# Hybrid attention and SSM block: attention's gate projection z moved from the head loop into two token-major passes

## The chip, the cores and the metric

The kernel runs on one core of one Trainium2 chip. The metric is the device time of one execution in microseconds; several runs are taken and their median is given. Beside it stands one profiled execution, whose trace is read here. Engines: PE is TensorE's matrix products, PEld its weight loads, DVE is VectorE, ACT is ScalarE, POOL is GpSimd, SP is SyncE, which issues most DMAs.

## The reference

One layer over 256 tokens of width 2048, in fp32. The normed input `hn` is projected by `w_in` to q, k, v, a gate `z_a`, and the inputs of a state-space branch (SSM). Attention has 16 heads of 128 with three dilated patterns and ALiBi slopes; the attended output is gated by `silu(z_a)` and projected.

```python
hn = rms_norm(x, norm_w)
proj = hn @ w_in
q, k, v, z_a, z_s, xbc, dt_raw, g_a, g_s = jnp.split(proj, split_points, axis=-1)
...
o_a = jnp.einsum('pbsh,pbshe->bshe', wts.astype(q.dtype), jnp.stack(outs))
o_a = o_a.reshape(b, s, ATTN_WIDTH) * jax.nn.silu(z_a)
...
y = rms_norm(y * jax.nn.silu(z_s), ssm_norm_w)
merged = jax.nn.sigmoid(g_a) * (o_a @ w_attn_branch) + jax.nn.sigmoid(g_s) * (y @ w_ssm_branch)
return x + merged @ w_out
```

A last RMS norm follows.

## The kernel before

**Precision by splitting.** Every fp32 operand of a large product is split into a high part (ScalarE copies it into the matmul's reduced format, `h`) and a low part (VectorE subtracts, `l`). A product is then high x high, high x low and low x high, accumulated in one PSUM bank. Weights come from HBM in units of 128 x 1024 fp32 (512 KB), in an order laid out by `weight_plan`; `unit` splits a unit (lines 278 and 279) into rings of four `h` and four `l` tiles, and the raw units have a ring of five. `XT` holds the transposed input with its high and low parts side by side (256 + 256 columns), 16 blocks (`KT`) of 128 rows.

**Two forms of projection.** `gemm_a` makes 128 output columns feature-major: the weight block is the stationary operand, `XT` streams. For each of the 16 blocks it issues one product of 512 columns (the high weight with both parts of the input, line 333) and one of 256 (the low weight with the high part, line 339). `gemm_pair` makes 1024 output columns token-major for both halves of the tokens: `XT` is stationary, weights stream 512 wide, and it works by quads, two blocks of 128 rows at a time. A plain quad has 24 products of 512 columns (lines 484 to 486, in `triple`). A quad listed in `S_QUADS` uses seven block products instead of eight (Strassen's way), 21 products, for which VectorE makes sums and differences of the weight blocks (`wt`, `wa`), unless an earlier "presum" job has put them in memory (`sum_jobs`: three markers on POOL, two loads on SP, two VectorE subtractions at lines 254 and 255, one store on SP). Products go to four banks of their own (`pp_`), the plain ones to four others (`ps_`), which swap between the passes c = 0 and c = 2; `fold` (lines 589 to 594) adds them together at the end.

**Stages, in order.** A first stage with the norm; eight SSM groups (xs, zs, B and C by `gemm_a`, with weight presums and left-operand sums made ahead); the SSM branch's output product (`ssm`, two `gemm_pair` passes); v (two passes); the loop over 16 heads; the gate `ga` (two passes); `attn` and `out` (two passes each); the last norm. In the head loop each head has three `gemm_a` projections, q, k and `za`. Their results are brought out of PSUM by `evac`, and `half_silu` makes the gate.

**The order of the work.** A clock of ticks (one for each projection, or each quad) says when the small steps are issued: `after(ticks, f)` puts a step on a list and `tick` runs what is due. For a head: `scores` (line 1051, then softmax on VectorE and ScalarE), `turn_p` (three 128x128 transposes of p on TensorE, line 1075), `mix` (p times v, lines 1082 and 1083, result feature-major, times the gate, split into `oaT`). A scheduler that simulates the engines puts the program's instructions in order; instructions marked with `in_order` keep theirs, among them the first and last product of each q, k and za projection. `oaT` is the left operand of `attn`; `keep_left` makes the sums of its seven-product quads.

**Memory.** Large areas are reused under tags: `yo0a`, `yo0b`, `yo1a`, `yo1b`. The SSM outputs `yT` lie in all four. During v, `yo0a` gives room for weight sums and `yo0b` for four extra split tiles (`tl`); `yo1b` becomes `th_a`, in which the attention stage's presum jobs work and later the gate `ga`.

Of the kernel before, what the change touches and what calls it, by code (L numbers as in the profile page):

```python
# [9 lines left out]
F32 = mybir.dt.float32  # L10
# [5 lines left out]
P = 128  # L16
S = 256
# [30 lines left out]
IN_TWOS = {(n, t) for n in ("xs", "zs") for t in range(4)} | {("B", 1), ("B", 4)} | {(n, h) for n in ("q", "k", "za") for h in range(2)}  # L48
# [35 lines left out]
def weight_plan():  # L84
# [114 lines left out]
def hybrid_block(ctx: ExitStack, tc: tile.TileContext, wall, xt, x, pk_d, cst_d, fw_d, out):  # L199
# [95 lines left out]
    def kt_of(t, kt):  # L295
        return t[kt // 8][:, kt % 8, :] if isinstance(t, list) else t[:, kt, :]

    def two_kts(t, q):
        t, q = (t[q // 4], q % 4) if isinstance(t, list) else (t, q)
        return t[:, 2 * q : 2 * q + 2, :]  # L300

# [135 lines left out]
    def fetch_left(kept, pool, bufs, key, x, spare, u, queue=nc.sync):  # L437
        def get(behind):
            sx = new_sx(pool, bufs, spare, f"{key[0]}{key[1]}")
            gp.tensor_copy(sx[:, 0, 0, 0:1], behind)  # L440
            queue.dma_start(sx.bitcast(F32), lefts[key])
            kept[key[1]] = left_parts(sx, x, spare)

        behind_unit(u, get)
# [24 lines left out]
    def gemm_pair(tag, x_of, n_kt, sxs, swap, extra={}, close=1, order=None, room={}, tail=None):  # L469
# [22 lines left out]
        for at, q in enumerate(order):  # L492
# [6 lines left out]
            if q not in quads:  # L499
# [8 lines left out]
                if tail and at == n_q - 1:  # L508
# [6 lines left out]
                for (ae, k, h, l), i, c, acc, cs, start, stop in jobs:  # L515
                    triple(acc, *ae[i][k], h[:, c, cs], l[:, c, cs], start=start, stop=stop and at == n_q - 1)
# [107 lines left out]

    yT = [half_kts(f"yT{n}", f"yo0{n}") for n in "ab"]
    ssq = cpool.tile([P, 2, S], F32, name="ssq", tag="ssq")
# [388 lines left out]

    def open_gate(c, es, prods):
        dst = blocks(th_a, c)
        fold(prods, dst)
        for d, e in zip(dst, es):
            ve.tensor_tensor(d, e, d, ALU.add)  # L1020
            ac.activation(d, d, AF.Tanh, scale=0.5)

    vt = big.tile([P, 2, D], F32, name="vt", tag="yo1a")
    th_a = big.tile([P, 2, D], F32, name="th_a", tag="yo1b")
    xl = ctx.enter_context(tc.tile_pool(name="xl", bufs=1))
# [18 lines left out]
    with tc.tile_pool(name="att", bufs=2) as ap:  # L1044
        ev = ap

        oaT = [half_kts("oaTa", "yo0a")]

# [28 lines left out]

        def mix(h, pT, za):
            ops = bank("m2", 2, f"ops{h}")
            o = za  # L1080
            hs = slice(h * P, (h + 1) * P)
            pe.matmul(ops[:, :S], vt[:, 0, hs], pT[:, :S], start=True, stop=False)
            pe.matmul(ops[:, P:S], vt[:, 1, hs], pT[:, S:384], start=False, stop=True)
            ve.tensor_tensor(o, ops[:, :S], za, ALU.mult)
            if h == 8:
                oaT.append(half_kts("oaTb", "yo0b"))
            split(o, kt_of(oaT, h)[:, :S], kt_of(oaT, h)[:, S:])
# [4 lines left out]
        sum_jobs(  # L1092
            SUMS_ATT, [FIRST[("q", 0)] + 3 + n * 15 // 4 for n in range(len(SUMS_ATT))],
            [
# [5 lines left out]
        for h in range(NH):  # L1100
# [5 lines left out]
            pT = ap.tile([P, 384], F32, name=f"pT{h}", tag="pT", bufs=1)  # L1106
            za = ap.tile([P, S], F32, name=f"za{h}", tag="za", bufs=3)
            after(S_LAG + (6, 4, 2)[max(h - 13, 0)], lambda a=(h, pT, za): mix(*a))
            after(S_LAG + (3 if h < 15 else 1), lambda a=(h, p, pT): turn_p(*a))
            after(S_LAG + (h == 0), lambda a=(h, q, k, p): scores(*a))  # L1110
            zh = ev.tile([P, S], F32, name=f"zah{h}", tag="eh", bufs=2)
            evac(project(("za", h)), zh, f"za{h}", scale=0.5)
            half_silu(zh, za, f"za{h}")

        for n, q in enumerate(ATT_QUADS):
            fetch_left(
                sx_of_o, xl if n else xk, max(1, n and len(SX_X) - 1), ("o", q), two_kts(oaT, q), 0, FIRST[("ga", 2)] + O_BEHIND[n], nc.gpsimd
            )
# [8 lines left out]
    with tc.tile_pool(name="fin", bufs=2) as fp:  # L1127
# [42 lines left out]

        fw = big.tile([P, D], F32, name="fw", tag="yo0b")
        for n, (tag, u) in enumerate(FW_BEHIND):
            cs = slice(n * UNIT, (n + 1) * UNIT)
            behind_unit(
                FIRST[tag] + u, lambda behind, cs=cs: fetch(fw[:, cs], fw_d[cs].partition_broadcast(P), behind, nc.scalar)
            )
# [9 lines left out]
        for c0 in (0, 2):  # L1186
# [17 lines left out]
            for i in range(2):  # L1204
                f = fs[:, i, :9]
                for c, acc in zip((c0, c0 + 1), es[2 * i : 2 * i + 2]):
# [17 lines left out]
                    if (c, i) == (2, 1):  # L1224
                        y2 = y
                    else:
                        ve.tensor_tensor(fin[:, i, cs], y, fw[:, cs], ALU.mult)
                    if c == 1:
# [7 lines left out]
        for i in range(2):  # L1236
            r = fs[:, i, 7:8]
            for c in (3, 0, 2, 1) if i else (3, 0, 1, 2):
                cs = slice(c * 512, (c + 1) * 512)
                if i and c == 2:  # L1240
                    ve.scalar_tensor_tensor(fin[:, i, cs], y2, r, fw[:, cs], ALU.mult, ALU.mult)
                elif c == 0 or c == (1 if i else 3):
# [40 lines left out]
```

## Time and profile before

| | |
|---|---|
| median of 3 runs | 1380.61 us (1380.14 to 1382.33) |
| profiled execution | 1379.87 us |
| its span | 1378.0 us |
| PE busy | 1366.8 us, 99% |
| DVE busy | 1177.0 us, 85% |
| ACT busy | 840.0 us, 61% |
| HBM | 252 GB/s over the span |

The span runs from the first to the last instruction of the trace. Matmuls are pipelined: the next starts before one has ended, so a duration in the trace is longer than the distance between two starts. The chain of waits is the chain of work that ended last, followed back from the last instruction; a piece of it is the time by which that instruction moved the end.

### The profile page before, as it was taken

The numbers are of one execution on the slowest core, as the hardware profiler recorded it, in microseconds if no ns is written. First come the engines' busy times: TensorE is split into PE (matmuls) and PEld (weight loads), VectorE is DVE, ScalarE is ACT, GpSimd is POOL, SyncE is SP. The second block draws the span as 40 slices with busy tenths as digits, with TensorE's granted clock in tenths as the row PEclk, the third lists the DMA queues.
The fourth block names the chain that finished last, engine by engine and source line by source line (L and its number), as shares of the span: only waits on it lengthen the run. The fifth ranks groups of instructions, "written<-read, shape, count | busy, mean of one in ns | idle before, by whom it ended". The sixth has DMA issues, their size and how long they took to land.

```text
span 1378.0 us, 20734 instructions
## 1 busy us (share of the span) xinstructions
PE 1366.8 (99%) x7260; PEld 1164.8 (85%) x7260; DVE 1177.0 (85%) x1763; ACT 840.0 (61%) x1310; POOL 161.7 (12%) x238
## 2 busy tenths in 40 slices
PE   9999999999999999999999999999999999999997
PEld 7888888888888888888888888888888888888886
DVE  6898899898899888788989888777877789988897
ACT  7655777675667676666565554454444557655564
POOL 2301211101020100010001001211211000400112
PEclk9999999999999999999999999999999999999999
DMA  9767878778787867578677568888889757875773
GB/s 342 237 190 237 298 267 286 262 244 288 248 277 237 298 203 220 174 242 277 228 261 270 211 215 316 306 275 280 306 298 302 230 163 267 291 244 173 246 273 122
DMA packets 106520, 348.15 MB, mean 253 GB/s; under 512 B 11888, under 2 KB 14256, under 8 KB 106416
## 3 DMA queue, kind: packets, MB, share of 16 engines
q1 hardware_dynamic: 104400, 340.67, 74.0%
q10 hardware_dynamic: 1440, 4.06, 0.8%
q0 software_dynamic: 576, 2.10, 0.4%
q8 instruction: 57, 0.93, 0.3%
q14 instruction: 47, 0.39, 0.1%
HBM read 316.97 MB, written 29.82 MB: 252 GB/s over the span
## 4 chain that ended last, share of the span: by engine, by line
PE 98%; DMA 0%; DVE 0%; ACT 0%; issue 0%; SPq 0%; POOL 0%; POOLq 0%; DVEq 0%
PE ps_xs L333 8%; PE ps_zs L333 8%; PE ps_k L333 4%; PE ps_za L333 4%; PE ps_q L333 4%; PE ps_zs L339 4%; PE ps_xs L339 4%; PE ps_ssm L485 3%; PE ps_ssm L486 3%; PE ps_ssm L484 3%; PE ps_q L339 2%; PE ps_za L339 2%; PE ps_k L339 2%; PE ps_gs L421 2%; PE ps_gs L422 2%; PE ps_gs L420 2%
## 5 line engine op out<-in xcount | busy, mean ns | idle before, releaser
L278 ACT ACTIVATE h<-w 128x1024 fp32r<-128x1024 f32 (+1 forms) x394 | 410.0, 1048 | 306.0 <-issue 73.7
L279 DVE TENSOR_TENSOR l<-w,h 128x1024 fp32r<-128x1024 f32 (+1 forms) x394 | 474.0, 1209 | 111.1 <-ACT h L278 106.9
L333 PE MATMUL ps_zs<-XT,h 128*128 128x512 f32 x496 | 172.0, 393 | 0.0
L333 PE MATMUL ps_xs<-XT,h 128*128 128x512 f32 x496 | 171.6, 393 | 0.0
L339 PE MATMUL ps_zs<-XT,l 128*128 128x256 f32 x496 | 134.6, 279 | 0.0
L339 PE MATMUL ps_xs<-XT,l 128*128 128x256 f32 x496 | 133.7, 277 | 0.0
L333 PEld LDWEIGHTS ps_xs<-XT,h 128*128 128x128 f32 x496 | 91.3, 188 | 19.4
L333 PEld LDWEIGHTS ps_zs<-XT,h 128*128 128x128 f32 x496 | 91.3, 188 | 18.9
L339 PEld LDWEIGHTS ps_zs<-XT,l 128*128 128x128 f32 x496 | 93.3, 188 | 2.1
L339 PEld LDWEIGHTS ps_xs<-XT,l 128*128 128x128 f32 x496 | 93.2, 188 | 2.1
L333 PE MATMUL ps_q<-XT,h 128*128 128x512 f32 x256 | 91.1, 404 | 0.0
L333 PE MATMUL ps_k<-XT,h 128*128 128x512 f32 x256 | 88.6, 395 | 0.0
L333 PE MATMUL ps_za<-XT,h 128*128 128x512 f32 x256 | 88.4, 394 | 0.0
L551 ACT ACTIVATE ha<-wa 128x1024 fp32r<-128x1024 f32 x45 | 47.5, 1056 | 45.9 <-PE ps_ssm L486 10.0
L339 PE MATMUL ps_q<-XT,l 128*128 128x256 f32 x256 | 68.4, 278 | 0.0
L339 PE MATMUL ps_k<-XT,l 128*128 128x256 f32 x256 | 68.4, 277 | 0.0
L339 PE MATMUL ps_za<-XT,l 128*128 128x256 f32 x256 | 68.4, 277 | 0.0
L552 DVE TENSOR_TENSOR la<-wa,ha 128x1024 fp32r<-128x1024 f32 x45 | 54.8, 1218 | 8.4 <-ACT ha L551 8.3
L552 DVE TENSOR_TENSOR ltu<-wa,htu 128x1024 fp32r<-128x1024 f32 x40 | 48.7, 1219 | 10.8 <-ACT htu L551 10.8
L793 ACT ACTIVATE gt<-acb,acT 128x128 f32<-128x128 f32 x128 | 44.1, 390 | 22.2 <-DMA acb<-acum_d 21.9
L333 PEld LDWEIGHTS ps_k<-XT,h 128*128 128x128 f32 x256 | 47.0, 188 | 9.9
L333 PEld LDWEIGHTS ps_q<-XT,h 128*128 128x128 f32 x256 | 47.1, 188 | 9.7
(691 smaller groups left out, 3347.8 us busy)
## 6 DMA issues: line engine op xcount, KB each, us to landing
w<-in_wall SPq DMA_DIRECT2D x390, 512.0 KB, 4.8
wa<-in_wall SPq DMA_DIRECT2D x45, 512.0 KB, 4.7
th_a<-in_wall SPq DMA_DIRECT2D x21, 512.0 KB, 4.7
sums_at<-in_wall SPq DMA_DIRECT2D x18, 512.0 KB, 5.0
acb<-acum_d SPq DMA_DIRECT2D x32, 256.0 KB, 3.8
t_ssm<-sums_at SPq DMA_DIRECT2D x13, 512.0 KB, 4.3
wt<-t_ssm SPq DMA_DIRECT2D x13, 512.0 KB, 4.7
th_a<-in_wall SPq DMA_DIRECT2D x21, 256.0 KB, 5.4
```

What stands on the lines that cost most here:

```text
L278: ac.activation(h[:, a:b], w[:, a:b], AF.Copy)
L279: ve.tensor_tensor(l[:, a:b], w[:, a:b], h[:, a:b].bitcast(F32), ALU.subtract)
L333: high = pe.matmul(acc, h[:, kk, :], xs_of(kt), start=(kt == 0), stop=False)
L339: low = pe.matmul(acc[:, S:], l[:, kk, :], xs_of(kt)[:, :S], start=False, stop=(kt == KT - 1))
L420: pe.matmul(accs[i], xh, h[:, kk], start=(kt == 0), stop=False)
L421: pe.matmul(accs[i], xh, l[:, kk], start=False, stop=False)
L484: pe.matmul(acc, xh, h, start=start, stop=False)
L485: pe.matmul(acc, xh, l, start=False, stop=False)
L486: pe.matmul(acc, xl, h, start=False, stop=stop)
L551: ac.activation(h, src, AF.Copy)
L552: ve.tensor_tensor(l, src, h.bitcast(F32), ALU.subtract)
L793: ac.activation(g4[:, n, b], acb[:, j, b // 2 * P : b // 2 * P + P], AF.Relu, scale=-1.0, bias=sc[:, h : h + 1],)
```

## The change

The z projection leaves the head loop. It becomes two `gemm_pair` passes of 1024 columns behind v (tag `za`, c = 0 and 2), each with two seven-product quads (2 and 5) without presums. At the end of a pass VectorE adds the banks, ScalarE takes the Tanh, and VectorE writes z(1 + tanh(z/2)) token-major into four tiles `za` of four heads each. In the head loop only q and k are projected. `mix` now takes p as the stationary operand and gives the output token-major, in three products of 128 columns; VectorE multiplies by the gate; a new step `turn_o` turns the two 128x128 blocks of the head by TensorE and splits the result into `oaT`. The four steps of a head have new ticks (`ATT_LAGS`).

Around it: quad 3 of the first ga pass becomes plain and the orders of quads change; six presum jobs of ga move from the head loop to the SSM groups (four jobs a group instead of three), 14 remain in the head loop; the area `yo0b` is cut into quarters, for `yTb`, three of the `za` tiles, the second half of `oaT` and `fw`; the extra split tiles `tl` move from `yo0b` to `yo1b`; `th_a` is allocated behind the z passes; a plain quad may run due steps half way.

```diff
+ATT_LAGS = (
+    ((2, 0), (5, 0), (6, 0), (7, 0)), ((2, 0), (4, 0), (5, 0), (6, 0)),
+    ((2, 0), (3, 0), (4, 0), (5, 0)), ((1, 1), (2, 1), (3, 0), (3, 1)),
+)
+Z_ORDERS = {c: (0, 2, 1, 3, 5, 4, 6, 7) for c in (0, 2)}
-G_ORDERS = {c: (0, 2, 4, 1, 3, 5, 6, 7) for c in (0, 2)}
+G_ORDERS = {0: (0, 1, 3, 2, 4, 5, 6, 7), 2: (0, 2, 4, 1, 3, 5, 6, 7)}
-    ("v", 0): (2, 3, 4, 5, 6), ("v", 2): (2, 4, 5, 6), ("ga", 0): (2, 3, 4, 5, 6), ("ga", 2): (2, 3, 4, 5, 6),
+    ("v", 0): (2, 3, 4, 5, 6), ("v", 2): (2, 4, 5, 6), ("za", 0): (2, 5), ("za", 2): (2, 5), ("ga", 0): (2, 4, 5, 6), ("ga", 2): (2, 3, 4, 5, 6),
+N_EARLY = 6
-SUMS_SSM = [(t, q) for t in (("ssm", 0), ("ssm", 2), ("v", 0), ("v", 2)) for q in S_QUADS[t] if (t[1], q) not in IN_PLACE.get(t[0], ())]
-SUM_UNITS = 2, 9, 16
+SUMS_SSM = [(t, q) for t in (("ssm", 0), ("ssm", 2), ("v", 0)) for q in S_QUADS[t] if (t[1], q) not in IN_PLACE.get(t[0], ())]
+SUMS_SSM += SUMS_ATT[:N_EARLY]
+SUM_UNITS = 2, 7, 12, 17
...
+    for c in (0, 2):
+        pair(("za", c), "w_in", OFF_ZA + c * 512, KT)
     for h in range(NH):
         cols(("q", h), "w_in", OFF_Q + h * P, KT)
         cols(("k", h), "w_in", OFF_K + h * P, KT)
-        cols(("za", h), "w_in", OFF_ZA + h * P, KT)
...
+                for at_job, ((ae, k, h, l), i, c, acc, cs, start, stop) in enumerate(jobs):
+                    if at_job == 4:
+                        run_due(now[0] + 0.5)
...
-    yT = [half_kts(f"yT{n}", f"yo0{n}") for n in "ab"]
+    yT = [half_kts("yTa", "yo0a"), [quarter("yTb", n) for n in range(4)]]
...
-    tl = big.tile([P, 4, UNIT], F32R, name="tl_v", tag="yo0b")
+    tl = big.tile([P, 4, UNIT], F32R, name="tl_v", tag="yo1b")
...
+        for c in (0, 2):
+            es, prods = gemm_pair(
+                ("za", c), lambda kt: XT[:, kt, :], KT, sx_of_x, c == 2, order=Z_ORDERS[c], room=room
+            )
+            tmp = [mul.tile([P, UNIT], F32, name=f"z_{t}{c}", tag=t, bufs=2) for t in ("ht", "lt")]
+            dst = [t[:, n * 512 : n * 512 + 512] for t in tmp for n in range(2)]
+            fold(prods, dst)
+            for n, (d, e) in enumerate(zip(dst, es)):
+                ve.tensor_tensor(d, e, d, ALU.add)
+                ac.activation(e, d, AF.Tanh, scale=0.5)
+                four = lambda t: t.rearrange("p (h m) -> p h m", h=4)
+                ve.scalar_tensor_tensor(za[c + n % 2][:, :, n // 2], four(e), 1.0, four(d), ALU.add, ALU.mult)
+        th_a = big.tile([P, 2, D], F32, name="th_a", tag="yo1b")
...
-            pe.matmul(ops[:, :S], vt[:, 0, hs], pT[:, :S], start=True, stop=False)
-            pe.matmul(ops[:, P:S], vt[:, 1, hs], pT[:, S:384], start=False, stop=True)
-            ve.tensor_tensor(o, ops[:, :S], za, ALU.mult)
+            pe.matmul(ops[:, :P], pT[:, :P], vt[:, 0, hs], start=True, stop=True)
+            pe.matmul(ops[:, P:S], pT[:, P:S], vt[:, 0, hs], start=True, stop=False)
+            pe.matmul(ops[:, P:S], pT[:, S:384], vt[:, 1, hs], start=False, stop=True)
+            o = za[h // 4][:, h % 4].rearrange("p i s -> p (i s)")
+            ve.scalar_tensor_tensor(o, ops[:, :S], 0.5, o, ALU.mult, ALU.mult)
+
+        def turn_o(h):
+            if h in (8, 10, 12, 14):
+                oaT[1].append(quarter("oaTb", h // 2 - 4))
+            tp = bank("m2", 2, f"otp{h}")
+            for i in range(2):
+                pe.transpose(tp[:, i * P : (i + 1) * P], za[h // 4][:, h % 4, i], ident)
+            split(tp[:, :S], kt_of(oaT, h)[:, :S], kt_of(oaT, h)[:, S:])
...
-            after(S_LAG + (6, 4, 2)[max(h - 13, 0)], lambda a=(h, pT, za): mix(*a))
-            after(S_LAG + (3 if h < 15 else 1), lambda a=(h, p, pT): turn_p(*a))
-            after(S_LAG + (h == 0), lambda a=(h, q, k, p): scores(*a))
-            zh = ev.tile([P, S], F32, name=f"zah{h}", tag="eh", bufs=2)
-            evac(project(("za", h)), zh, f"za{h}", scale=0.5)
-            half_silu(zh, za, f"za{h}")
+            for (ticks, inside), f in zip(ATT_LAGS[max(h - 12, 0)], ...):
+                after(ticks, f, inside)
```

More of the change, by code (lines that the diff above doesn't have):

```diff
@@ L1045, in hybrid_block, with open_gate @@
         ev = ap
-        oaT = [half_kts("oaTa", "yo0a")]
+        za = [
+            big.tile([P, 4, 2, P], F32, name=f"za{n}", tag=f"yo0b{n}") if n < 3
+            else ap.tile([P, 4, 2, P], F32, name=f"za{n}", tag="za", bufs=1)
+            for n in range(4)
+        ]
+        for c in (0, 2):
[11 more added lines that the diff above has]
+        th_a = big.tile([P, 2, D], F32, name="th_a", tag="yo1b")
+        oaT = [half_kts("oaTa", "yo0a"), []]
+        def open_gate(c, es, prods):
+            dst = blocks(th_a, c)
+            fold(prods, dst)
+            for d, e in zip(dst, es):
+                ve.tensor_tensor(d, e, d, ALU.add)
+                ac.activation(d, d, AF.Tanh, scale=0.5)
         def scores(h, q, k, p):
@@ L1106, in hybrid_block @@
             pT = ap.tile([P, 384], F32, name=f"pT{h}", tag="pT", bufs=1)
[L1107 to L1113 removed]
+            for (ticks, inside), f in zip(
+                ATT_LAGS[max(h - 12, 0)],
+                (
+                    lambda a=(h, q, k, p): scores(*a), lambda a=(h, p, pT): turn_p(*a),
+                    lambda a=(h, pT): mix(*a), lambda h=h: turn_o(h),
+                ),
+            ):
+                after(ticks, f, inside)
         for n, q in enumerate(ATT_QUADS):
             fetch_left(
[L1117 removed]
+                sx_of_o, xl if n else xk, max(1, n and len(SX_X) - 1), ("o", q), lambda q=q: two_kts(oaT, q), 0, FIRST[("ga", 2)] + O_BEHIND[n], nc.gpsimd
             )
@@ L1169, in hybrid_block, with fw @@
             )
-        fw = big.tile([P, D], F32, name="fw", tag="yo0b")
+        fws = [big.tile([P, UNIT], F32, name=f"fw{n}", tag=f"yo0b{n}") for n in range(2)]
+        def fw(c):
+            return fws[c // 2][:, c % 2 * 512 : c % 2 * 512 + 512]
         for n, (tag, u) in enumerate(FW_BEHIND):
```

35 lines of the change are left out of this document (15 added, 20 removed).

## The prediction

> **What bounds the kernel now.** I read the profile in this order: the page's engine totals and its chain, then the busy time by stretch, then the chain of waits piece by piece where TensorE does the work that the change replaces, and last VectorE's groups and waits in the stages that get more work.
>
> ```profile
> span 1378.0 us, 20734 instructions
> PE 1366.8 (99%) x7260; PEld 1164.8 (85%) x7260; DVE 1177.0 (85%) x1763; ACT 840.0 (61%) x1310; POOL 161.7 (12%) x238
> PE 98%; DMA 0%; DVE 0%; ACT 0%; issue 0%; SPq 0%; POOL 0%; POOLq 0%; DVEq 0%
> 30.00:1360.00 1330.00, 1329.98 (x7072) 1133.51 (x7071) 1144.12 (x1709) 811.68 (x1257) 152.38 (x216) 1.00 0.76 253
> 165.00:225.00 60.00, 60.00 (x368) 52.12 (x366) 57.62 (x97) 42.91 (x82) 9.83 (x18) 1.00 0.85 289
> 225.00:285.00 60.00, 60.00 (x368) 52.08 (x366) 55.50 (x95) 42.06 (x80) 9.51 (x16) 1.00 0.80 271
> 744.00:822.00 78.00, 78.00 (x345) 64.36 (x344) 70.79 (x75) 44.54 (x51) 4.07 (x5) 1.00 0.62 212
> 895.64:913.92 18.28, 18.28 (x109) 16.09 (x108) 13.03 (x26) 8.97 (x14) 3.99 (x4) 1.00 0.82 286
> ```
>
> The lower rows give stretch, its length, then busy time of PE, PEld, DVE, ACT and POOL, granted clock, DMA share, GB/s. The fourth row is the one to see: from 30 to 1360 us TensorE is idle for 0.02 us, at clock 1.00. Busy PE alone could hide a slow pace, but the chain also runs along PE for 98% of the span. So no wait is there to be removed. The change can win only by giving TensorE less work, and can lose by more work or a new wait. VectorE is next: 96% busy in the second SSM group (165 to 225), 91% in v (744 to 822), 71% in one head (895.64 to 913.92).
>
> **What z costs now.** The chain, in order of time (start, length, what), over the z projection of one head and the attention work that follows:
>
> ```profile
> 926.82 0.23 PE ps_za L333
> ...
> 932.24 0.12 PE ps_za L339
> 932.36 0.43 PE ops L1082 x2
> 932.79 0.22 PE ops L1083 x2
> 933.01 0.33 PE ptp L1075 x3
> 933.34 0.22 PE sps L1051 x2
> 933.57 0.43 PE sps L1052 x2
> 934.00 0.23 PE ps_q L333
> ```
>
> One z projection lasts from 926.82 to 932.36, 5.54 us for 16 products of 512 columns and 16 of 256. Then come mixing (ops, 0.65), three turns of p (0.33) and the scores (0.65). A head takes 18.28 us: three times 5.54 plus 1.64. Removed: 16 x 5.54 = 88.64 us.
>
> **What z costs as two passes.** The v passes have the form that z gets. Their chain, over a run of plain products:
>
> ```profile
> 783.17 0.23 PE ps_v L484
> 783.39 0.23 PE ps_v L485
> 783.62 0.23 PE ps_v L486
> ...
> 789.74 0.23 PE ps_v L486
> 789.97 0.23 PE pp_v L484
> ```
>
> From 783.17 to 789.97 are 30 products: 0.2267 us each. A plain quad has 2 x 2 x 2 x 3 = 24 of them, a seven-product quad 7 x 3 = 21. A z pass has eight quads, two with seven: 6 x 24 + 2 x 21 = 186; two passes 372 products, 84.33 us. Gain 4.31 us, of which the 12 saved products are 2.72 and the rest is that two 256-column products take longer than one of 512.
>
> **What comes back.** Quad 3 of the first ga pass goes from seven products to plain: 3 x 0.2267 = +0.68. Mixing has three 128-wide products instead of a 256-wide and a 128-wide one: 3 x 0.22 against 0.65, 16 x 0.01 = +0.16. And each head turns two 128x128 blocks:
>
> ```profile
> L1075 PE MATMUL ptp<-cst,p 128*128 128x128 f32 x48 | 8.0, 273 | 0.0
> 118.86 0.88 PE xtp L813 x8
> 118.69 0.17 PE lastb L753 x2
> L333 PE MATMUL ps_q<-XT,h 128*128 128x512 f32 x256 | 91.1, 404 | 0.0
> L333 PE MATMUL ps_za<-XT,h 128*128 128x512 f32 x256 | 88.4, 394 | 0.0
> ```
>
> In the chain three turns take 0.33 and eight 0.88, so 0.11 us each: 32 x 0.11 = +3.52. The duration column says 273 ns, but that is one turn from start to end; its neighbours run inside it. The lower end is the smaller neighbour, 0.085 each (lastb), 0.8 us less in all; the upper end is the whole 273 ns, 32 x 0.163 = 5.2 us more. I take 0.11, the same instruction on the same shape. The Trainium skill (TensorE: Matmul & The Clock Gate, Part 4: PE-mode transpose) puts a 128x128 turn at about 275 ns in a kernel's context and speaks against this change; by it the sum below would be 5.2 us higher. The trace agrees with the figure as a duration and not as a price in a stream.
>
> Each head also gets a second seam between the projections and fp32 work, since the four attention steps are spread over two ticks. The seam above is filled to 0.01 us (1.63 of 1.64), so I take nothing; the upper end is the difference between the first projection behind a seam and a later one, (404 - 394) ns x 16 = 0.16 us, 2.6 us over 16 new seams.
>
> PE's sum: -88.64 + 84.33 + 0.68 + 0.16 + 3.52 = +0.05 us. **The gain is used up by the turns and the lost quad.** What decides is whether a wait appears.
>
> **The other engines.** Prices:
>
> ```profile
> L279 DVE TENSOR_TENSOR l<-w,h 128x1024 fp32r<-128x1024 f32 x36 | 44.0, 1222 | 18.9 <-ACT h L278 18.7
> L254 DVE TENSOR_TENSOR th_a<-th_a 128x512 f32<-128x512 f32 x10 | 6.9, 691 | 1.5 <-POOL th_a L253 0.9
> L255 DVE TENSOR_TENSOR th_a<-th_a 128x512 f32<-128x512 f32 x9 | 6.2, 685 | 0.1
> L395 DVE SCALAR_TENSOR_TENSOR zah<-ps_za,lo_za 128x256 f32<-128x256 f32 x6 | 2.5, 417 | 0.0
> L405 DVE SCALAR_TENSOR_TENSOR za<-th_za,zah 128x256 f32<-128x256 f32 x6 | 2.5, 413 | 0.0
> L1021 ACT ACTIVATE th_a<-th_a 128x512 f32<-128x512 f32 x8 | 4.9, 624 | 4.4 <-DVE th_a L1020 4.4
> SPq L250 <- POOL sums_at L249: 42.1, 21, 3.3
> ```
>
> Heads: a head becomes 18.28 - 5.54 + 0.22 + 0.01 = 12.97 us. VectorE loses 2 x 1.222 + 0.417 + 0.413 = 3.27 us, and the weight sums are 14 in 64 weight units instead of 21 in 96 (0.9 a head instead of 1.3, at 0.691 + 0.685), 0.6 less. 13.03 - 3.9 = 9.1 of 12.97, 70% where it was 71%. Turns of p and mixing are now one tick (about 6.5 us) apart, with one copy of ScalarE between; mixing and the turns of o too, with one VectorE product between. The scores keep their three ticks. No charge.
>
> z passes: a plain quad costs VectorE 2 x 1.222, a seven-product quad without a presum three 512-wide and four 1024-wide operations, 3 x 0.69 + 4 x 1.222 = 6.96. 12 x 2.44 + 4 x 6.96 + 24 x 0.69 for closing two passes = 73.7 of 84.3 us, 87%, less than v's 91%. New is that the accumulators of a z pass come free only after an add, a Tanh and a product (0.69 + 0.624 + 0.69), where v needs the add alone; the second pass wants these banks at its second quad, 5.4 us later. In line on VectorE, eight 0.69 and a Tanh are 6.1 us after the pass, though three quarters of them can start earlier, since the last quad closes the four accumulators one after the other. Queued behind them are the splits of the second pass; if these go first the banks wait for 6.96 more, 13.0 in all against about 7.5 allowed (5.4 and the three products before the next of these banks is wanted, 2.0): up to 5.5 us. Ends 0 and 5.5; v's own handover, nearest in form, shows no PE idle, so I take 0.3.
>
> SSM: six weight sums move here, four per group instead of three, 6 x 1.38 = 8.3 us on VectorE, 12 DMAs in and 6 out on SP, 18 markers on POOL, 1.25 MB a group beside some 17 (289 GB/s x 60 us). In the fullest group 57.62 + 1.38 = 59.0 of 60 us. SP's queue waits for POOL's marker of a sum 21 times, up to 3.3 us now (the last row: total, times, longest), behind which the next weight load stands; the ring of five weight tiles of 2.8 us each covers that. Ends 0 and 8.3; ScalarE still waits for PE to free weight buffers in these groups (next fence), so the splits run ahead: I take 0.
>
> Start of v: the tile `tl`, into which the first seven-product quad splits its sums, moves to the memory of the last SSM outputs, which TensorE reads until 744.25.
>
> ```profile
> ACT h L278 <- PE ps_zs L333: 4.9, 5, 1.5
> L551 ACT ACTIVATE tl_v<-room_v x3: 1044/1044/1063, 720.8 to 768.4; 128x1024 fp32r<-128x1024 f32 x3
> 743.65 1.49 DVE L1013 TENSOR_TENSOR tmp_lt<-ps_ssm,tmp_lt 128x512 f32<-128x512 f32 x2
> 745.65 1.22 DVE L552 TENSOR_TENSOR la<-wa,ha 128x1024 fp32r<-128x1024 f32 x1
> 750.34 1.23 DVE L552 TENSOR_TENSOR tl_v<-wa,tl_v 128x1024 fp32r<-128x1024 f32 x1
> 750.37 0.39 PE L484 MATMUL pp_v<-tl_v,sx_x 128*128 128x512 f32 x1
> ```
>
> Its first split ran at 720.8 and is used at 750.37; now it can start only behind 744.25, with ScalarE's following splits queued behind it, and its 1.22 us on VectorE push the later ones, of which the last (750.34 to 751.57) is just in time. Ends 0 and 1.2; I take 0.3, as the order of products can be turned a little. The rest (quarter tiles, `fw` in halves) moves no instruction: nothing.
>
> **Sum:** 1378.0 + 0.05 + 0.6 = 1378.65 us of span; the profiled execution took 1379.87 with 1.87 outside its span, so 1380.5; the median of the runs, 1380.61, lies 0.74 above that execution, so 1381.2.
>
> **Rivals.**
> (a) VectorE's handover between the z passes (or at v's start) stops TensorE: 1380.7 + 5.5 = 1386.2. It decides against "no change" once banks come free 2.8 us too late. For it: the chain of three operations per bank and unpresummed quads; against: products of the third, plain quad can go ahead. 0.13.
> (b) VectorE bounds the SSM groups: nothing of the 8.3 us is hidden, 1389.0; it decides when a third of it shows. For it: 98% in one group; against: the later groups (55.5 of 60) and the buffers ahead. 0.07.
> (c) The turns cost their whole duration: 1385.9. Against: 0.33 for three. This is the time that the skill's figure gives. 0.04.
> (d) Faster: the turns cost TensorE nothing and only the 4.31 - 0.68 - 0.16 remain: 1377.1. Against: both rows of the chain show them in line. 0.07.
>
> **How the numbers follow.** 0.2% of 1380.61 is 2.8 us, about what can be told from no change. My forecast, with waits under 2.8 us, has 0.69; the rivals (a) to (c) make 0.24 slower, (d) 0.07 faster. Range: below, 1381.2 less the 0.6 taken, 0.8 (turns at 0.085), 0.5 (lowest run shown) and 0.8 for rounded pieces of the chain, 1378.5; above, to (a) with 0.8 for v's start, 1387.0. Left out are most of (b) and (d).
>
> **What would show it.** The chain still 98% PE; no `ps_za` at L333; z products at 0.227 us with 372 of them; heads 12.97 us apart; turns of o at 0.22 a head. PE idle between 30 and 1360 us is the wait that I take as 0.6: look at 744 to 757, at the middle of z (42 us behind its start), at the SSM groups and at the first ga quads. I am wrong if heads are longer than 13.2 us, or if PE is idle for 3 us in one place.

## The result and the profile after

The changed kernel is slower: 1403.57 us (median of 4 runs, 1402.3 to 1406.28) against 1380.82 us (1380.14 to 1382.33), a ratio of 1.0168, 95% interval 1.0156 to 1.018. The prediction was 1381.2 us, 1378.5 to 1387.0, with 0.69 on "no change": wrong, by some 22 us and outside the range. The profiled execution of the changed kernel is its slowest run, 1406.28 us, so the trace shows 26.4 us to explain where the medians differ by 22.8.

The page's engine totals and chain:

```profile
span 1404.5 us, 20568 instructions
PE 1377.3 (98%) x7187; PEld 1166.4 (83%) x7187; DVE 1188.9 (85%) x1770; ACT 837.9 (60%) x1296; POOL 158.1 (11%) x235
PE 78%; DMA 4%; DVE 3%; issue 2%; ACT 2%; POOL 1%; SPq 0%; POOLq 0%; DVEq 0%; ACTq 0%
```

TensorE still carries the end, but the chain leaves it for a fifth of the span, over DMAs, VectorE and ScalarE. First, is TensorE's sum as predicted? The chain of waits from one head to the next:

```profile
978.02 0.33 PE ptp L1110 x3
...
990.77 0.22 PE otp L1127 x2
990.99 0.33 PE ptp L1110 x3
```

From one turn of p (978.02) to the next (990.99) are 12.97 us, the predicted head to the hundredth; two turns of o cost 0.22, 0.11 each. So the sum of +0.05 us stands. The time went into waits. Waits of TensorE between 30 and 1390 us (in total, times, longest); before, the same view of 30 to 1360 us has no row:

```profile
PE xtp L831 <- DVE xs L418: 7.5, 1, 7.5
PE pp_v L497 <- ACT tl_v L566: 3.3, 1, 3.3
PE ps_ga L497 <- ACT h L286: 2.1, 1, 2.1
PE ps_v L497 <- ACT h L286: 1.1, 1, 1.1
PE pp_ga L497 <- ACT ha L566: 0.9, 1, 0.9
PE ps_za L497 <- ACT h L286: 0.9, 1, 0.9
PE ps_gs L434 <- DVE l L287: 0.9, 1, 0.9
PE pp_ga L497 <- ACT htu L566: 0.2, 1, 0.2
```

They sum to 16.9 us. The rest, some 9.5 us, is products that follow each other more slowly. Behind the three longest waits run stretches of 5.0, 3.4 and 3.3 us at a granted clock of 0.50, which cost half their length, some 6 us. The stretches (length, busy time of PE, PEld, DVE, ACT, POOL, granted clock, DMA share, GB/s) show the three places; the last row is 2 us within the slow stretch behind the longest wait:

```profile
165.00:225.00 60.00, 52.52 (x294) 45.48 (x291) 54.12 (x93) 37.31 (x74) 10.64 (x19) 0.91 0.84 275
756.00:841.00 85.00, 79.67 (x340) 64.27 (x339) 71.12 (x76) 45.23 (x51) 12.21 (x5) 0.98 0.57 191
1134.00:1220.00 86.00, 82.74 (x368) 66.51 (x367) 72.01 (x92) 50.80 (x64) 3.60 (x6) 0.98 0.68 218
186.00:188.00 2.00, 2.00 (x9) 1.81 (x8) 2.00 (x6) 1.24 (x4) 0.00 (x0) 0.50 0.70 260
```

The split by stage comes from the first products of v and ga in the timeline, first before, then after:

```profile
744.25 0.39 PE L484 MATMUL ps_v<-h,XT 128*128 128x512 f32 x1
...
1116.45 0.58 PE L484 MATMUL ps_ga<-h,XT 128*128 128x512 f32 x1
```

```profile
756.18 0.39 PE L497 MATMUL ps_v<-h,XT 128*128 128x512 f32 x1
...
1134.55 0.48 PE L497 MATMUL ps_ga<-h,XT 128*128 128x512 f32 x1
```

- Ahead of v: 756.18 - 744.25 = +11.9 us, of which 10 in the second SSM group (the wait of 7.5 and 2.5 for the slow products behind it), and most of the rest near 315 us (a wait of 0.9).
- v, z and heads: +6.2 us, where TensorE's own work should give -0.6 and another -1.7 (the last heads' turns, scores and mixing now lie inside the ga pass: 3.3 us of them at the prediction's prices, where there were 1.6): some 8.4 us of waits and slow products, nearly all in v.
- From ga to the end of the span: 269.95 - 261.55 = +8.4, less 0.7 for the lost quad and those 1.7: some 6 us of waits and slow products, in the first ga pass.

Three places, then, near 12, 8 and 6 us. The experiments take them one by one. "The ga sum" below is the time from each ga product to TensorE's next instruction, added over the 357 products: 81.3 before (354 products), 88.7 after.

### The profile page after: what moved, and what is told of

Its sections match the earlier page's. It is cut to its first block, busy times and chain, and to the rows that moved or that the text cites. A ratio compares the mean times of both kernels' runs of the same rounds, so it can differ in the third digit from the quotient of the medians.

```text
span 1404.5 us, 20568 instructions
## 1 busy us (share of the span) xinstructions
PE 1377.3 (98%) x7187; PEld 1166.4 (83%) x7187; DVE 1188.9 (85%) x1770; ACT 837.9 (60%) x1296; POOL 158.1 (11%) x235
## 4 chain that ended last, share of the span: by engine, by line
PE 78%; DMA 4%; DVE 3%; issue 2%; ACT 2%; POOL 1%; SPq 0%; POOLq 0%; DVEq 0%; ACTq 0%
PE ps_xs L346 6%; PE ps_zs L346 6%; PE ps_q L346 4%; PE ps_k L346 4%; PE ps_zs L352 3%; PE ps_xs L352 3%; PE ps_ssm L498 3%; PE ps_ssm L499 3%; PE ps_ssm L497 3%; PE ps_k L352 2%; PE ps_q L352 2%; PE ps_za L497 2%; PE ps_za L498 2%; PE ps_za L499 2%; PE ps_C L346 2%
## 5 line engine op out<-in xcount | busy, mean ns | idle before, releaser
L286 ACT ACTIVATE h<-w 128x1024 fp32r<-128x1024 f32 (+1 forms) x388 | 402.7, 1047 | 304.3 <-issue 100.3
L287 DVE TENSOR_TENSOR l<-w,h 128x1024 fp32r<-128x1024 f32 (+1 forms) x388 | 465.7, 1208 | 90.8 <-ACT h L286 87.8
L566 ACT ACTIVATE ha<-wa 128x1024 fp32r<-128x1024 f32 x48 | 50.8, 1058 | 67.8 <-PE ps_v L499 15.1
L567 DVE TENSOR_TENSOR la<-wa,ha 128x1024 fp32r<-128x1024 f32 x48 | 58.5, 1220 | 11.6 <-ACT ha L566 11.4
L566 ACT ACTIVATE htu<-wa 128x1024 fp32r<-128x1024 f32 x41 | 43.2, 1053 | 14.8 <-PE ps_ssm L499 5.2
L352 PEld LDWEIGHTS ps_k<-XT,l 128*128 128x128 f32 x256 | 48.4, 189 | 1.8
```

What stands on the lines that cost most here:

```text
L286: ac.activation(h[:, a:b], w[:, a:b], AF.Copy)
L287: ve.tensor_tensor(l[:, a:b], w[:, a:b], h[:, a:b].bitcast(F32), ALU.subtract)
L352: low = pe.matmul(acc[:, S:], l[:, kk, :], xs_of(kt)[:, :S], start=False, stop=(kt == KT - 1))
L566: ac.activation(h, src, AF.Copy)
L567: ve.tensor_tensor(l, src, h.bitcast(F32), ALU.subtract)
```

## The experiments

All times are medians with the kernel before beside them on the same chip (1380.6, 1379.95, 1380.13, 1381.24 and 1380.4 in the five groups of runs).

### The SSM group

The changed kernel, ScalarE's wait for `acb` (the decays, a tile with one buffer) between 140 and 190 us:

```profile
ACT gt L811 <- DMA acb<-acum_d: 7.2, 3, 3.3
```

VectorE there, in brackets the idle time before its instruction and what ended it, and the chain of waits from POOL's markers of a sum job to the wait of TensorE:

```profile
158.21 1.23 DVE L287 TENSOR_TENSOR l<-w,h 128x1024 fp32r<-128x1024 f32 x1 [4.25 <-ACT h L286]
```

```profile
138.92 2.05 POOL sums_at L257 x2
...
142.30 6.90 DMA acb<-acum_d
...
151.12 4.51 DMA acb<-acum_d
...
157.23 0.96 ACT h L286
...
171.05 5.70 DMA acb<-acum_d
...
184.49 0.43 DVE xs L418
184.96 1.97 PE xtp L831 x8
```

The job of 138.92 is the third of the four. Its two loads (768 KB, issued at 140.87) stand in SP's queue ahead of an `acb` load (142.30), which lands 6.90 us later. ScalarE, in order, waits for it; the next `acb` load can go only when ScalarE has read the last one (151.12); ScalarE's split of a weight tile stands behind that second wait, and VectorE idles 4.25 us for the split. POOL's marker of the fourth job starts only after that split too (158.30), and SP, which issues nothing from 153.6 to 159.5, stands for this marker. Busy time of VectorE from 140 to 160 us (stretch, length, then PE, PEld, DVE), before, then after:

```profile
140.00:160.00 20.00, 20.00 (x117) 17.63 (x116) 16.82 (x22) 15.19 (x30) 5.30 (x6) 1.00 0.78 268
140.00:160.00 20.00, 20.00 (x117) 17.66 (x116) 12.48 (x18) 13.96 (x32) 2.79 (x7) 1.00 0.73 253
```

VectorE is idle there for 7.5 us where it was idle for 3.2, is then all but full from 160 to 190 us (29.17 of 30) and delivers `xs` late. The kernel before waits for `acb` as well (6.3 us in four waits, the longest 2.5), so the wait by itself is not new, but its length is. Two theories: the queue (SP, its markers and its loads), or VectorE's load (rival (b)).

**e1: three jobs again in the first two groups that have jobs, and the two that are left over in group 7** (the "second group" is `g == 1`).

```diff
-            SUMS_SSM, [FIRST[("B", g)] + n for g in range(1, 7) for n in SUM_UNITS],
+            SUMS_SSM, [FIRST[("B", g)] + n for g in range(1, 8) for n in (SUM_UNITS if 2 < g < 7 else (2, 9, 16))],
```

> The changed kernel loses TensorE time in three places: about 10 us in the second SSM group (165 to 190 us), about 8 us in v (760 to 845), about 6 us in the first ga pass (1160 to 1205). Here the same 24 early presum jobs are made, but SSM groups 1 and 2 have three each as before the change (units 2, 9, 16), groups 3 to 6 four, and group 7 three (of which two are left over for jobs). Queue theory (the fourth job's POOL marker holds SP's in-order queue in the group where the left-operand sums are also made, so the broadcast of the decays and the weights come late): the 7.6 us wait of the turn of xs goes, 1393 to 1395 us, v and ga as they were. Rival (VectorE is simply full): VectorE's busy time is moved by 1.4 us out of a group of 60, so no more than 1.4 us a group, at least 1401.

Measured: 1393.27, ratio 1.0092 (1.0077 to 1.0107); 10.3 us faster than the changed kernel. The wait at `xtp` is gone, and TensorE is busy without a gap from 140 to 330 us.

**e9: the kernel before, with the early sums alone** (six ga presums in the SSM groups, four jobs a group; the head loop's 15 jobs spaced five units).

```diff
+N_EARLY = 6
+SUMS_SSM += SUMS_ATT[:N_EARLY]
-SUM_UNITS = 2, 9, 16
+SUM_UNITS = 2, 7, 12, 17
```

> One part of the change alone: the kernel before, with z still in the head loop, but with six presum jobs of ga moved to the SSM groups, four a group at units 2, 7, 12, 17. If the fourth job is the whole cause of the SSM loss, the turn of xs waits here too: 1380.3 + 9 to 12 = 1389 to 1392 us, all of it between 165 and 190 us. If the quarter tiles or another part of the change is needed for it, 1379 to 1382.

Measured: 1392.15, ratio 1.0091 (1.0074 to 1.0108), and the same wait in the trace, 7.8 us:

```profile
PE xtp L815 <- DVE xs L407: 7.8, 1, 7.8
...
```

With e1 this is the SSM part from both sides: the fourth job a group costs 10 to 12 us, with or without the rest of the change. Its place matters less:

**e10: with e4's edit (below), the second job of the second group at unit 9 instead of 7.** `SUM_UNITS` for g = 1 becomes `(2, 9, 13, 17)`.

> The changed kernel with the split tiles of v in their old place (e4_tl_back, 1398.7), four presum jobs in every group, but in group 1 at units 2, 9, 13, 17 instead of 2, 7, 12, 17. In group 1 the first left operand of x is also made at unit 7. If the meeting of the two at unit 7 is the cause (a place, not a count), the SSM wait goes: 1387 to 1389. If four jobs are too many for that group, 1397 to 1400.

Measured: 1395.76 (1393.85 to 1402.85), ratio 1.0124; its base e4 has 1398.72. The profiled execution is the slowest of its runs and still has a wait of 6.6 us at `xtp`; the other three runs, 1393.85 to 1396.40, are 2 to 5 us below e4. So the meeting of two jobs at one unit is not the whole cause.

**e12, e13, e14: what of the fourth job.** All on e4. In e12 the third job of that group issues its DMAs and markers but no additions; in e13 it adds but has no markers, loads and store; in e14 that group's markers are made by ScalarE.

```diff
 e12  -            ve.tensor_tensor(res[:, :512], ...)            (and the second; SUMS_SSM[2] only)
 e13  -            gp.tensor_copy(dst[:, 0:1], behind); nc.sync.dma_start(dst, src)   (the same job)
 e14  -            gp.tensor_copy(dst[:, 0:1], behind)
 e14  +            (ac.copy if (tag, q) in SUMS_SSM[:4] else gp.tensor_copy)(dst[:, 0:1], behind)
```

> The changed kernel with the tile tl of v in its old memory, and in the second SSM group the third of the four sum jobs issues its markers, loads and store but not its two VectorE subtractions of 128x512 (0.68 us each; that one product sum is left out, its memory holds an older sum). Queue theory (the wait of 7 us before xtp at 177 to 185 comes from SP standing behind the markers, and so from the late acb loads): the wait stays, 1397 to 1400 (the same kernel with the subtractions 1398.7). VectorE theory (VectorE is full from 160 to 190 us and the extra 1.4 us a job decides): the wait falls below 2 us, 1387 to 1391.

> The mirror of the last: the same job keeps its two subtractions (on the loads of the job before) but has no markers, loads and store (that product sum is left out). Queue theory: the wait before xtp falls below 2 us, 1387 to 1391. VectorE theory: it stays, 1397 to 1400.

> The changed kernel with tl in its old memory and the markers of the four sum jobs of the second SSM group by ScalarE, 12 x some 0.2 us there, in place of POOL. If POOL's slow markers (1 to 3 us each) hold SP: the wait falls below 3 us, 1388 to 1392. If SP's order, the bytes or VectorE's load decide, whatever engine marks: it stays, 1396 to 1400; some new wait by ScalarE's own order can add 1 to 2.

Measured: 1394.64, 1390.22 (1386.64 to 1392.87) and 1394.13, against 1398.72 for e4. TensorE's waits between 140 and 330 us, in e12, then in e14; e13's profiled execution has none (it is the fastest of its runs, so others of them may have one):

```profile
PE xtp L832 <- DVE xs L419: 4.9, 1, 4.9
...
```

```profile
PE xtp L831 <- DVE xs L418: 3.6, 1, 3.6
PE ps_zs L352 <- DVE l L287: 2.1, 1, 2.1
```

Neither pure theory holds. Without the additions (1.4 us of VectorE's time) 4.1 us go, and a wait of 4.9 stays with VectorE less loaded; without markers, loads and store 8.5 go; with the markers on another engine 4.6, and a new wait of 2.1 appears in a later group. The trace of e13 fits the chain above: without the third job's loads ahead of it the `acb` load of 141.36 is used at 145.63, 4.3 us later instead of 6.9, and VectorE is idle for 3.2 us from 140 to 160 us, as in the kernel before. So what the job puts into the queue is the larger part, and VectorE's load, which leaves no slack to make up for it, is the smaller. Whether the markers or the bytes of the loads count for more is not separated by e13, and the scheduler plans the order anew in each of the three. Since the parts overlap I don't add them.

### The start of v

The changed kernel's timeline from a marker on POOL for a left-operand load to TensorE's wait, with VectorE's last instruction of an unbroken row (the chain of waits runs over the same steps):

```profile
765.04 8.83 POOL L453 CAST sx_x<-h 128x1 fp32r<-128x1 f32 x2 [11.73 <-ACT h L286]
772.50 1.22 DVE L580 TENSOR_TENSOR wa<-wa,room_v 128x1024 f32<-128x1024 f32 x1
773.78 0.33 SPq L454 DMA_DIRECT2D sx_x<-sxd_x  x1
775.15 0.38 SPq L548 DMA_DIRECT2D room_v<-t_v  x1
781.41 1.06 ACT L566 ACTIVATE htt<-room_v 128x1024 fp32r<-128x1024 f32 x1 [11.15 <-DMA room_v<-t_v]
783.47 0.52 PE L497 MATMUL pp_v<-tl_v,sx_x 128*128 128x512 f32 x1 [3.32 <-ACT tl_v L566]
```

The first of these two one-column casts takes 8.71 us (the second, behind it, 0.18), and SP's queue waits for it 9.4 us, with the presum's load (775.15) behind. VectorE's instructions show beside what: from 757.60 on they are subtractions and additions of two SBUF tiles without a gap, and the cast ends as the row of them does (772.50 + 1.22 = 773.72). In the e4 run the same two markers take 1.24 and 0.48 us:

```profile
765.70 1.23 DVE L287 TENSOR_TENSOR l<-w,h 128x1024 fp32r<-128x1024 f32 x1 [0.22 <-ACT h L286]
765.73 1.24 POOL L453 CAST sx_x<-h 128x1 fp32r<-128x1 f32 x1 [12.18 <-ACT h L286]
767.62 0.48 POOL L453 CAST sx_x<-h 128x1 fp32r<-128x1 f32 x1 [0.66 <-ACT h L286]
770.67 1.23 DVE L567 TENSOR_TENSOR ltt<-room_v,htt 128x1024 fp32r<-128x1024 f32 x1 [0.34 <-ACT htt L566]
```

The Trainium skill (SBUF — State Buffer, section "Who interferes with whom") says that a VectorE instruction with two SBUF inputs contends with a GpSimd instruction that reads SBUF, the loser blocking until the other is done. The trace agrees, and in the changed kernel the marker was blocked through a whole row of such instructions and not through one. That is not so every time: in e4 both markers ended between 765.70 and 770.33, where VectorE's row of such instructions has no gap. What lets a marker in is not shown.

**e2: the markers of these four loads by ScalarE** (`fetch_left(..., mark=ac.copy)`). **e4: `tl` of v back in its old memory**, so that its first split can run early and VectorE's order is another one; z's `tl` stays in `yo1b`.

```diff
 e2  -            gp.tensor_copy(sx[:, 0, 0, 0:1], behind)
 e2  +            mark(sx[:, 0, 0, 0:1], behind)
 e4  -    tl = big.tile([P, 4, UNIT], F32R, name="tl_v", tag="yo1b")
 e4  +    tq = [quarter("tl_v", n).rearrange("p k m -> p (k m)") for n in range(4)]
```

> The marker writes of the four late left operands at the start of v are made by ScalarE instead of POOL; nothing else is edited. Lock-out theory (one POOL write of 128 x 1 took 8.7 us, from 765.0 until VectorE's first gap at 773.7, and SP stood behind it, so weights and presums came 9 us late): the 3.5 us wait at 783 us and the slow clock behind it go, 4 to 6 us less, 1398 to 1400. Rival (the move of the split tiles behind the last SSM product makes VectorE late): nothing changes, 1402 to 1405.

> The extra split tiles of v lie again in the memory that they had before the change (its quarters), those of the z passes in the new place. Nothing else is edited. If the move of these tiles is what fills VectorE without a gap from 749 to 773.7 us and so locks POOL's marker out, the wait at 783 us goes as in the run with the marker on ScalarE: 1398 to 1400. If the lock-out comes from the rest of v's start (the marker would be as late as before): 1402 to 1405.

Measured: e2 1403.3, no gain; e4 1398.72, ratio 1.0131 (1.0114 to 1.0148), 4.8 us faster. In e2 the wait of 3.3 in v is gone too, but a new one of 3.1 stands in the fourth SSM group (`ps_zs`, for VectorE's `l`), where these runs are near the edge.

**e8: e1 and e2 together; e5: e1 and e4 together**, to see the v part without the SSM one.

> SSM groups 1 and 2 with three presum jobs, and the four markers of v written by ScalarE, the split tiles in the changed place. e2_marker_scalar took away the 3.5 us wait in v but another wait of 3.3 us came in the fourth SSM group. With the SSM groups relieved, lock-out theory: 1393.3 - 5 = 1388 us, as e5_three_tl. If the split tiles themselves cost: 1391 or more.

> Both edits that helped, together: SSM groups 1 and 2 with three presum jobs, and the split tiles of v in their old place. If the two stalls are separate, the gains add: 1393.3 - 4.9 = 1388.4 us, with what is left of the loss in the first ga pass (about 4 us) and at the start of z (about 1.5). If the VectorE-full theory holds, the work only moves and the gain is less than 2 us: 1391 or more.

Measured: 1387.61, ratio 1.0056 (1.0041 to 1.0071), and 1387.41, 1.0053 (1.0038 to 1.0068). Against e1 (1393.27) the marker's engine alone gives 5.7 us, the memory of `tl` 5.9: the same wait taken away in two ways that share nothing but the marker's delay. (The kernel before ran 0.65 us faster beside e5 and e8 than beside e1, so both gains are rather 5 us.) In e8 `PE pp_v` is gone from TensorE's waits.

### The first ga pass

What stays at 1387.4 is some 7 us, most of it here. Four theories: a burst of loads of attn's first presums (into the tile `fin`), four seven-product quads in a row, the last heads' work in the pass, and a queue on ScalarE.

**e3: hold those loads (`fin`, 1.5 MB) to a unit of the second pass.** The unit chosen lies in a seven-product quad, which serves no holds, so the edit had no effect: the run repeats the changed kernel. **e6: the same on e5, to a plain quad's unit.**

```diff
+                        behind_unit(FIRST[("ga", 2)] + FIN_AT, lambda behind, i=i, at=at: gp.tensor_copy(fin[:, i, at : at + 1], behind))
```

> The loads of attn's first presums into the final buffer are held until unit 7 of the second ga pass; in the changed kernel four of them (1.5 MB) were issued at 1160 us in the middle of the first ga pass, as soon as the last head had been mixed, just ahead of a weight load that landed after 7.7 us. Theory (burst in front of the weights): the 2.2 us wait at 1171 us and the slow clock behind it go, 4 to 6 us less, 1398 to 1400. Rival (the shorter ticks at the end of the heads make scores, turns and splits bunch on VectorE and ScalarE in ga's first quads, and SP's queue stood still from 1137 to 1145 us for that reason): at most 1 us less.

> e5_three_tl, with the loads of attn's first presums held until unit 3 of the second ga pass (in e3_fin_late the hold was put on a unit of a seven-product quad, which calls no hooks, so that run repeats the changed kernel). Burst theory: the wait of a plain product for its weights near the end of the first ga pass goes, 3 to 4 us less than e5_three_tl. Rival (bunching of four seven-product quads in a row and the last head's softmax on VectorE and ScalarE): within 1 us of e5_three_tl.

Measured: 1405.43 for e3; e6 1391.08, ratio 1.0071, 3.7 us slower than e5. The old wait went from 2.0 to 1.4; a new one of 5.5 appeared (`pp_ga`, for ScalarE's `ha`), behind four markers that POOL again took 8.8 us for, 8.41 of them for the first:

```profile
1177.61 8.77 POOL L1170 COPY fin<-h 128x1 f32<-128x1 f32 x4 [88.37 <-ACT h L287]
```

So e6 moves the burst but puts another delay in its place, and the burst is not ruled out: in the changed kernel's chain of waits the weight load with which TensorE's wait of 2.06 us ends was issued right behind four such loads (1159.97 to 1161.29).

```profile
1162.27 7.70 DMA w<-in_wall
...
1170.05 1.06 ACT h L286
```

**e7, e11, e15: the order of the quads, on e5.** In e7 a plain quad stands between two pairs; e11 has only three seven-product quads; e15 has the five and the order of the kernel before.

```diff
 e5   ("ga", 0): (2, 4, 5, 6)       G_ORDERS[0] = (0, 1, 3, 2, 4, 5, 6, 7)
 e7   ("ga", 0): (2, 4, 5, 6)       G_ORDERS[0] = (0, 1, 2, 4, 3, 5, 6, 7)
 e11  ("ga", 0): (4, 5, 6)          G_ORDERS[0] = (0, 1, 2, 4, 3, 5, 6, 7)
 e15  ("ga", 0): (2, 3, 4, 5, 6)    G_ORDERS[0] = (0, 2, 4, 1, 3, 5, 6, 7)
```

> e5_three_tl, with the first ga pass in the order 0, 1, 2, 4, 3, 5, 6, 7, so that a plain quad stands between the seven-product quads (two and two, not four in a row). Bunching theory: the small waits of 0.4 us for split sums and the wait of the last plain quad go, 2 to 4 us less than e5_three_tl. Burst theory: the loads for attn come as before, no change, or later, since the last head's output now waits for the banks of the pass, and then the gain is the same for another reason: the trace tells (where the loads of attn's presums stand).

> e5_three_tl (1387.4) with three instead of four seven-product quads in the first ga pass, in the order 0, 1, 2, 4, 3, 5, 6, 7: three more products (0.68 us), 5.6 us of VectorE less in the stretch that holds the last head's softmax. Bunching theory: of the 5.7 us that the ga passes lose, at least 3 come back, 1383.5 to 1385.5. If the waits come from something else (burst of loads for attn): 1387 to 1389.

> The kernel with both known waits taken away (three sum jobs in groups 2 and 3, tl in its old memory, 1387.4), with the five seven-product quads and the order of the first ga pass of the kernel before (2 and 4, one plain, 3, 5 and 6). TensorE has three products fewer, 0.7 us. If four such quads in a row make the pass wait: ga from 87.7 to below 83, 1383 to 1385. If the work of the last head, which now runs inside this pass, makes it wait whatever the order: ga stays over 85.5, 1386 to 1388.

Measured: 1386.59, 1387.06, 1386.91; ga sums 85.0 (357 products), 86.0 (360) and 87.3 (354), where e5 has 87.7 (357). e15 puts the kernel before's own order into the new surroundings and keeps some 7 us above the pure pace (354 x 0.2267 = 80.3); there this order had one. So order alone isn't it: the surroundings make the pass late. One candidate is a row of ScalarE, at the start of the pass in the changed kernel (ga begins at 1134.55), and the same copy in the kernel before:

```profile
1139.59 0.49 ACT L1111 ACTIVATE pT<-ptp 128x384 f32<-128x384 f32 x1 [4.16 <-PE ptp L1110]
```

```profile
1116.18 0.49 ACT L1076 ACTIVATE pT<-ptp 128x384 f32<-128x384 f32 x1 [0.20 <-PE ptp L1075]
```

The copy of head 14's turned p stands in ScalarE's order ahead of the pass's splits, but TensorE makes that turn only 4.5 us into the pass. ScalarE stands 4.16 us with the splits behind it, where it stood 0.20. Against it: the chain of waits does not run over this copy but along TensorE until 1149.85, and e15, as slow, has no such wait at this copy.

**e16 (on e5) and e17 (on e7): that wait taken away.** The turns of head 14's p and head 13's o are left out, and ScalarE handles columns of `XT` of the same size.

```diff
-            ac.activation(pT, tps[:, :384], AF.Copy)
+            ac.activation(pT, tps[:, :384] if h != 14 else XT[:, 0, :384].bitcast(F32), AF.Copy)
```

> The kernel with both known waits taken away (1387.4). At the start of the first ga pass its ScalarE stands 4.2 us at the copy of head 14's turned p, whose turn TensorE reaches only 19 products into the pass, and the splits of that pass stand behind it. Here the turns of p of head 14 and of o of head 13 are left out, and ScalarE copies and splits columns of XT in their place (128x384 and 128x256, as many elements), so nothing on ScalarE waits for TensorE there; the order of the pass is planned anew. If this queue is what the pass waits for: no wait of ScalarE over 2 us in the first 10 us of the pass, ga from 87.7 to below 84.5, 1382.5 to 1384.5, of which the five turns left out are 0.6. If the pass waits for weights, for VectorE or for the four quads in a row whatever happens at its start: ga stays over 86, 1386 to 1388.

> The same with the plain quad 3 between the seven-product quads (without the edit 1386.6 and ga 85.0). Queue theory: ga near 82, 1382 to 1384. The others: 1385.5 to 1387.

Measured: e16 1389.04, a miss (ga 86.2); e17 1382.55, ratio 1.0018 (1.0008 to 1.0027), ga 83.4. TensorE's waits in that pass, e5, then e17:

```profile
PE ps_ga L497 <- ACT h L286: 2.0, 1, 2.0
...
```

```profile
PE ps_ga L498 <- DVE l L287: 0.5, 1, 0.5
...
```

Each edit alone does little or harm (against the kernel before e5 has 1.0053, e7 1.0049, e16 1.0064); both together reach 1.0018, 4.9 us below e5, of which the five turns left out are 0.6. That looks as if the pass's waits needed both, late splits and four quads in a row. But the edit did not free ScalarE: in e16 and e17 the wait of 4.16 is gone and one split (`htt`) comes 4.5 us earlier, and a wait for VectorE stands behind that split. Here it is in e17, whose pass begins at 1118.52:

```profile
1123.98 0.63 ACT L294 ACTIVATE sxt_o<-sxt_o 128x512 fp32r<-128x512 f32 x1 [3.22 <-DVE sxt_o L474]
```

The next split of a weight sum (`ha`) comes 7.1 us into the pass in e17, and 7.0 in e7. So e17's gain cannot be put down to ScalarE's queue alone. The scheduler also orders the pass anew in e16 and e17. What makes this pass late is therefore not shown, and why e16 came out slower than e5 is open too.

No version beats the kernel before: the best that computes everything is e7 with 1386.59, and since TensorE's sum is unchanged, taking away all waits would only bring its time back.

## Why the prediction was wrong

**Right: TensorE's sum.** Heads of 12.97 us, turns at 0.11 each in the stream, 0.2267 us a product, no second-seam cost. e17, with most waits gone, has 1382.55, less than 2 us from the forecast's 1381.2, with five turns fewer. Rival (c), the turn at its whole duration, and (d) are out.

**Right: the handover between the z passes**, taken at 0.3: no wait stands in the middle of z. Rival (a), the likeliest on my list, did not happen; a wait of 0.9 us at the start of z, which I did not name, did (in the other runs up to 1.5, within the first 15 us of z).

**Wrong: the SSM term, taken as 0, measured 10 to 12 us.** I gave 8.3 us as its upper end, the whole of VectorE's added work. I charged work to an engine and looked for its slack over 60 us (59.0 of 60), and wrote off SP's wait for markers because the ring of weight tiles covers it. What isn't covered by that ring are the loads of `acb` in the same queue, which carry the chain of waits; e13 shows the job's markers, loads and store as the larger part, e12 the additions as the smaller. It is rival (b) by its place, not by its mechanism (VectorE first stood idle and only then was full), and above its price: the wait of 7.5 us was followed by 5 us of products at half pace (clock 0.50), some 2.5 us lost.

**Wrong: the start of v, taken as 0.3, upper end 1.2, measured some 8.** I named the moved `tl` and followed it to VectorE's order, where I priced it by VectorE's own lateness. The harm came through a marker on POOL that I did not follow: beside VectorE's row of two-tile operations it took 8.71 us, and SP's queue stood with it.

**Wrong: "No charge" for the heads' new ticks, and no price for the ga pass, measured 4 to 6.** That step looked at the distance from producer to consumer within a head and not at the end of the loop, where 3.3 us of the last heads' work, and the steps of the other engines that belong to it, now lie inside the next pass. Which of them makes the pass late stays open: the order of its quads alone does not (85.0 to 87.3 in e7, e11 and e15, where e5 has 87.7), and e6, e16 and e17 do not separate the rest.

Common to the first two: I added up busy time and asked for slack, but the loss sits in an in-order queue where a short instruction waits, or a large load goes ahead, and urgent loads stand behind it. The signs announced in the prediction (TensorE idle 3 us in one place; the SSM groups, 744 to 757 us and the first ga quads as places to look) were the right ones, but the sum allowed 0.6 us for all of them, and the range only one of them at a time.

## What to carry to other kernels

Where TensorE never waits, an edit that leaves its work unchanged can only lose, so price the queues and not only the engines: for every instruction that is added or moved, list what stands behind it in SP's, POOL's and ScalarE's order, and how long that can wait. Read the chain of waits first: a long wait that the chain does not run over, such as ScalarE's 4.16 us, need not cost anything. A one-column marker on POOL can take as long as a whole row of VectorE operations beside it (8.71 us here); put markers whose queue carries urgent loads on another engine. And find the stage's true slack by an experiment of the cheap part alone (here the early sums, e9) before building the rest.

## What the hardware showed that I had not expected

- One 128x1 cast on POOL took 8.71 us, and one 128x1 copy in e6 8.41 us, beside a row of VectorE operations on two SBUF tiles without a gap. Other such markers take 0.2 to 1.24 us, two of them in e4 beside such a row. The kernel before has one of 6.20 us too (1187.62), and TensorE does not wait there.
- Behind a wait of 7.5 us a 512-column product of TensorE took 0.43 us to the next start instead of 0.23, at a granted clock of 0.50, until 189.9 us, 5 us after the wait had ended. The Trainium skill (TensorE: Matmul & The Clock Gate, Part 1) has the half clock after an idle window of some 3.4 us. In the ga pass a wait of only 2.06 us (1169.1 to 1171.16) was followed by such a stretch too, beginning 1.8 us after the wait (granted clock 0.50 from 1173 to 1176):

```profile
1171.16 0.98 PE L497 MATMUL ps_ga<-h,XT 128*128 128x512 f32 x3 [2.06 <-ACT h L286]
...
1173.30 0.63 PE L498 MATMUL ps_ga<-l,XT 128*128 128x512 f32 x1
1173.72 0.63 PE L499 MATMUL ps_ga<-h,XT 128*128 128x512 f32 x1
```

So a wait can cost more than its length, and less than 3.4 us of it can be enough. It need not: in e5 a wait of 1.99 us was followed by none (granted clock 1.00 from 1153 to 1165).
